# VectorE splits the routing's weights, the paced queue of GpSimd holds only issues, and the second half of the one-hot tables moves into the first pass over V

## The chip, the cores and the metric

The kernel runs on one core of one Trainium2 chip. Its engines are TensorE (PE, matmuls), VectorE (DVE), ScalarE (ACT), GpSimd (POOL) and SyncE (SP, which issues most DMAs). Each engine takes its own instructions strictly in the order in which the program was built, and waits for others by semaphores. The metric is the device time of one execution in microseconds, lower is better.

## The reference, cut to what matters

Two layers. Each has a token mixer (three attentions, projections), which the change leaves alone, and then PEER, the retrieval of experts, which holds all of the change. There are 512 latent tokens and 256 context tokens (tiles of 128 tokens: 0 to 3 latent, 4 and 5 context); the second layer computes the latent tokens alone.

```python
def peer(h, wq, subkeys, u, v):
    q = (h @ wq).reshape(t, 8, 2, 128)
    s = einsum('thpd,hpnd->thpn', q, subkeys)          # 128 row scores, 128 column scores
    s_top, i_top = top_k(s, 16)
    ...                                                # 16 best of the 16 x 16 sums, for each head
    gate = softmax(best)
    a = gelu(einsum('cd,chkd->chk', hc, u[ec]))        # u, v: 16384 x 1024
    w = gc * a
    return einsum('chk,chkd->cd', w, v[ec])
```

Each token picks 8 x 16 = 128 of 16384 experts. The kernel doesn't gather 128 rows of V for a token: it makes, for each tile of tokens, a dense table of weights (16384 experts x 128 tokens, zero where an expert is not picked) and multiplies it with all of V.

## The kernel before

**Stages of a layer's PEER.** (1) The first pass over U (`upass`, half 0, matmuls into `pw`): 64 iterations, each loads a block of 128 experts (512 KB), splits it into two float16 parts (ScalarE the high one, VectorE the low one, tile `hl`), and multiplies it with the tokens of the *dense* tiles: 24 matmuls of 512 columns in layer 0 (tiles 2, 3, 4, 5), of 384 in layer 1 (tiles 2, 3, 1). Beside it run the routing (`routing`: 32 blocks of queries a layer, `rw`, whose weights `wq` and `sk` are scaled and split in `wsplit`) and the choice of experts (`pick`, with 128 small VectorE instructions `gjk` a tile that has a table). (2) The second pass over U (half 1, into `pa`), 64 iterations of the same. (3) Two passes over V (`vpass`, into `acc`), 128 iterations each, for three tiles in layer 0 (18 matmuls of 512 columns an iteration) and two in layer 1 (12). V too is split into two `hl` parts, one iteration ahead of its use.

**Three kinds of work fill the passes**, put into each iteration by generators at hand-written rates (`RRATE` for the routing, `RATES` for the gathers, `SRATES` for the scatters, by layer and stage):
- *Gathers* (`gather`, L946): tiles that are not dense (0 and 1 in layer 0, 0 in layer 1) fetch their 128 picked rows of U for every token. GpSimd issues 128 indirect DMAs a tile (512 KB each, into one of three buffers `r`), and VectorE multiplies each row with the tokens' `h` and sums it (L952).
- *Scatters* (`Table.put`, L1248): the weights of tiles 4, 5, 0, 1 (layer 0) and 0, 1 (layer 1) go into their table in HBM by 128 indirect DMAs a tile from GpSimd, 16 for each head; the next head's wait until they have landed. The table must be full before the pass over V that reads it (`need`).
- *One-hot blocks* (`Onehot.block`): the weights of tiles 2 and 3 are made on the chip. 32 blocks for each half of the columns; a block is three VectorE instructions (`oi`, `oj`, `og`), 16 small matmuls, and for half 0 a VectorE product into `P`, for half 1 two ScalarE copies into `P`. Before, all 64 run in the second pass over U, one an iteration.

**What sets the order.** A scheduler places all instructions on the engines' queues by its own estimates of time and by the program's order. `queue_behind` adds an edge without a semaphore: a gather or scatter may not stand before `lo_ins`, the last split that GpSimd did. When the routing's last split has been written, `lo_ins` stays where it is, and nothing more holds the issues back.

In `gather`, `h` is copied by ScalarE into PSUM (`hp`), and the products are summed in `a` (two buffers).

## Time and profile before

| | us |
|---|---|
| median of 3 runs | 5107.54 (5106.78 to 5112.42) |
| the profiled execution | 5100.45 |
| its span, first instruction to last | 5098.7 |
| PE busy | 4160.3 (82%) |
| DVE busy | 3334.4 (65%) |
| ACT busy | 1935.6 (38%) |
| POOL busy | 1776.3 (35%) |

The busy shares are means over stages with different limits: where one engine is busy all the time another may be idle, and the stage's own rows say which. POOL's issue of an indirect DMA counts as busy; the transfer itself runs on the DMA engines afterwards.

### The profile page before, as it was taken

What the parts mean: (1) busy time and instruction counts of PE and PEld (TensorE: products, weight loads), DVE (VectorE), ACT (ScalarE), POOL (GpSimd) and SP (SyncE); (2) the same over time, 40 slices, a digit from 0 to 9 for tenths busy, and PEclk for the clock granted to TensorE, in tenths of its full rate; (3) what the DMA queues carried; (4) which work ended last, traced back from release to release, by engine and by line L of the source; (5) the groups of instructions that cost most, each with busy time, mean ns of one, the idle gap of its engine ahead of it and who ended that gap; (6) DMA issues with size and microseconds to landing.
All of it is one profiled execution on the core that took longest, in us unless ns stands there. A gap on an engine that the chain in (4) does not pass through costs nothing. (4 is left out here: it accounts for less than half of the span.)

```text
span 5098.7 us, 74857 instructions
## 1 busy us (share of the span) xinstructions
PE 4160.3 (82%) x27326; PEld 2297.0 (45%) x27326; DVE 3334.4 (65%) x7769; ACT 1935.6 (38%) x3191; POOL 1776.3 (35%) x1680
## 2 busy tenths in 40 slices
PE   4987898981687777799899989878866587899898
PEld 3664554740343333344344456646543354444343
DVE  6677559691786666655565544654976587667565
ACT  4556343420122222233333346644432123455444
POOL 3224133477456676620000012333257645400000
PEclk9996899995898889899999999879988798999999
DMA  7831443321477788897788842134543477668787
GB/s 254 298 102 34 150 131 98 116 76 31 153 250 247 250 281 262 272 324 239 241 265 257 252 134 81 43 113 138 172 144 116 143 238 254 226 218 254 254 274 237
DMA packets 512322, 971.54 MB, mean 191 GB/s; under 512 B 73824, under 2 KB 295488, under 8 KB 511952
## 3 DMA queue, kind: packets, MB, share of 16 engines
q1 hardware_dynamic: 422464, 759.66, 46.2%
...
HBM read 861.77 MB, written 104.78 MB: 190 GB/s over the span
## 5 line engine op out<-in xcount | busy, mean ns | idle before, releaser
L1126 PE MATMUL acc<-hl,gst 128*128 128x512 f16 x7680 | 1710.7, 385 | 152.5 <-DVE hl L1114 105.8
L1126 PEld LDWEIGHTS <-gst 128*128 128x128 f16 x7680 | 760.6, 99 | 1101.9 <-issue 217.9
L952 DVE SCALAR_TENSOR_TENSOR r<-r,hp 128x1024 f32<-128x1024 f32 x384 | 466.2, 1218 | 580.0 <-DMA r<-peer_u,ix 579.4
L1113 ACT ACTIVATE hl<-s 128x1024 f16<-128x1024 f32 x512 | 538.0, 1051 | 698.5 <-PE acc L1126 392.2
L1114 DVE TENSOR_TENSOR hl<-s,hl 128x1024 f16<-128x1024 f32 x512 | 626.3, 1224 | 244.8 <-ACT hl L1113 243.4
L946 POOL DMA_INDIRECT r<-peer_u,ix x384 | 421.9, 1099 | 488.9 <-DVE r L952 339.5
L168 PE MATMUL pa<-h2Uh,hl 128*128 128x512 f16 (+1 forms) x1024 | 384.2, 376 | 192.9 <-DVE hl L143 192.8
L160 POOL TENSOR_TENSOR rstd<-rstd,mhalf 128x1 f32<-128x1 f32 x26 | 14.2, 546 | 1352.1 <-DVE rstd L159 1348.2
L1248 POOL DMA_INDIRECT table<-a,to x384 | 428.9, 1117 | 149.7 <-issue 110.7
L1248 POOL DMA_INDIRECT table<-gs,to x384 | 410.4, 1069 | 188.1 <-issue 108.8
L168 PE MATMUL pw<-h2Uh,hl 128*128 128x512 f16 (+1 forms) x1024 | 376.4, 368 | 67.1 <-DVE hl L143 67.0
L143 DVE SCALAR_TENSOR_TENSOR hl<-s,hl 128x1024 f16<-128x1024 f32 x256 | 313.7, 1226 | 172.0 <-ACT hl L139 172.0
L168 PEld LDWEIGHTS <-hl 128*128 128x128 f16 x2048 | 209.9, 102 | 477.9 <-DVE hl L143 272.3
L166 PE MATMUL pa<-h2Uh,hl 128*128 128x512 f16 (+1 forms) x1024 | 387.8, 379 | 8.7 <-ACT hl L139 8.7
L166 PE MATMUL pw<-h2Uh,hl 128*128 128x512 f16 (+1 forms) x1024 | 376.9, 368 | 14.0 <-ACT gst L1054 13.7
L167 PE MATMUL pa<-h2Ul,hl 128*128 128x512 f16 (+1 forms) x1024 | 385.7, 377 | 0.0
L167 PE MATMUL pw<-h2Ul,hl 128*128 128x512 f16 (+1 forms) x1024 | 375.7, 367 | 0.0
L153 POOL TENSOR_TENSOR wl<-wst,wh 128x512 f16<-128x512 f32 x96 | 127.9, 1344 | 504.4 <-ACT wh L152 468.5
L167 PEld LDWEIGHTS <-hl 128*128 128x128 f16 x2048 | 210.8, 103 | 205.2 <-issue 52.8
L166 PEld LDWEIGHTS <-hl 128*128 128x128 f16 x2048 | 210.8, 103 | 204.5 <-issue 39.1
L168 PE MATMUL pj<-wh,hTl 128*128 128x256 f16 x1072 | 295.7, 276 | 1.9 <-DVE hTl L141 1.6
L166 PE MATMUL pj<-wh,hTh 128*128 128x256 f16 x1072 | 295.8, 276 | 1.3 <-ACT hTh L139 1.3
...
## 6 DMA issues: line engine op xcount, KB each, us to landing
s<-peer_v SPq DMA_DIRECT2D x512, 512.0 KB, 4.7
s<-ut SPq DMA_DIRECT2D x256, 512.0 KB, 4.1
...
wq<-peer_wq SPq DMA_DIRECT2D x128, 256.0 KB, 3.6
...
```

Source lines behind the costliest of these rows:

```text
L143: nc.vector.scalar_tensor_tensor(lo, src, scale, hi, op0=OP.mult, op1=OP.subtract)
L153: self.lo_ins = nc.gpsimd.tensor_tensor(lo, w, hi, op=OP.subtract)
L160: nc.gpsimd.tensor_tensor(r, r, self.mhalf[:, :w], op=OP.pow)
L166: nc.tensor.matmul(out, ah, bh, start=start, stop=False)
L167: nc.tensor.matmul(out, ah, bl, start=False, stop=False)
L168: nc.tensor.matmul(out, al, bh, start=False, stop=stop)
L946: self.queue_behind(nc.gpsimd.indirect_dma_start(out=r, out_offset=None, in_=self.i["peer_u"], in_offset=bass.IndirectOffsetOnAxis(ap=ix[: ...
L952: nc.vector.scalar_tensor_tensor(r, r, 1.0, hp, op0=OP.mult, op1=OP.mult, accum_out=a[:, d // 16, d % 16:d % 16 + 1])
L1113: nc.scalar.activation(vh[:, 0], v, AF.Copy)
L1114: nc.vector.tensor_tensor(vh[:, 1], v, vh[:, 0], op=OP.subtract)
L1126: nc.tensor.matmul(acc[s][hf], pr[:, w, s, j % 2], vh[:, x, hf * 512:hf * 512 + 512], start=j == 0 and i == 0, stop=j == 127 and i == 2)
L1248: ins = o.nc.gpsimd.indirect_dma_start(out=self.d, out_offset=bass.IndirectOffsetOnAxis(ap=to[:, k, h:h + 1], axis=0), in_=values[:, c + s ...
```

## The change

- `wsplit` takes an engine for the low part. The routing's low parts (`wql`, `skl`) go from GpSimd to VectorE. In the first 24 iterations of the first pass over U (`UPOOL`), the low part of U goes from VectorE to GpSimd, with one more ScalarE instruction that scales U.
- `lo_ins` is now the low split of U or V of each iteration, on whichever engine, so it moves on through all passes.
- `Onehot.blocks(half)`: half 0 is made in the second pass over U, one block in two iterations; half 1 in the first pass over V, one block in two iterations, until iteration 62.
- `h` of a gather stays in SBUF (`hg`), without the copy into PSUM; `a` and `hg` have one buffer each. The second pass over U has two PSUM buffers for four, `wq` two buffers for four, `sk` two for three, `oi` and `og` one for two. In layer 0's second pass over V both vectors of the next layer's `ada` stand in `r` buffers, before one stood in PSUM.
- New rates.

```diff
-RATES = {0: (1.0, 1.4, 1.4, 1.4, 0.0, 0.0), 1: (1.0, 1.0, 0.8, 0.8, 0.0, 0.0)}
-SRATES = {0: (2.5, 2.6, 1.7, 2.2, 4.0, 4.0), 1: (2.5, 2.5, 1.4, 1.6, 4.0, 4.0)}
-RRATE = (1.2, 1.0)
+RATES = {0: (0.8, 1.0, 1.5, 1.5, 0.0, 0.0), 1: (0.6, 1.2, 0.4, 0.8, 0.0, 0.0)}
+SRATES = {0: (2.0, 2.9, 1.6, 1.8, 4.0, 4.0), 1: (1.5, 1.8, 0.9, 1.2, 4.0, 4.0)}
+RRATE = (1.3, 1.05)
...
+UPOOL = 24
...
-        self.lo_ins = nc.gpsimd.tensor_tensor(lo, w, hi, op=OP.subtract)
+        return (lo_eng or nc.gpsimd).tensor_tensor(lo, w, hi, op=OP.subtract)
...
-            sk = pool.tile([128, 128], F32, name="sk", bufs=3)
+            sk = pool.tile([128, 128], F32, name="sk", bufs=2)
...
-            self.wsplit(skh, skl, sk, SKS)
+            self.wsplit(skh, skl, sk, SKS, lo_eng=nc.vector)
...
-                w = pool.tile([128, 4, 128], F32, name="wq", bufs=4)
+                w = pool.tile([128, 4, 128], F32, name="wq", bufs=2)
...
-                self.wsplit(wh, wl, w)
+                self.wsplit(wh, wl, w, lo_eng=nc.vector)
...
-        h = self.gp.tile([128, D], F32, name="r")
+        h = self.lp.tile([128, D], F32, name="hg", bufs=1)
         nc.scalar.dma_start(h, self.h2d[t])
-        hp = self.hpp.tile([128, D], F32, name="hp")
-        nc.scalar.activation(hp, h, AF.Copy)
-        a = self.lp.tile([128, 8, 16], F32, name="a", bufs=2)
+        a = self.lp.tile([128, 8, 16], F32, name="a", bufs=1)
...
-                nc.vector.scalar_tensor_tensor(r, r, 1.0, hp, op0=OP.mult, op1=OP.mult,
+                nc.vector.scalar_tensor_tensor(r, r, 1.0, h, op0=OP.mult, op1=OP.mult,
...
-            ps = self.pool(e, "ups", 4, space=PSUM)
+            ps = self.pool(e, "ups", 2, space=PSUM)
...
-                vec = [self.srow(r(), 0, self.hpp.tile([128, D], F32, name="hp")), self.srow(r(), 1)]
+                vec = [self.srow(r(), x) for x in range(2)]
...
-        steps = iter(self.onehot) if half else iter(())
+        steps = self.onehot.blocks(0) if half else iter(())
...
-            self.split(uh[:, 0], uh[:, 1], u, US)
+            if not half and jj < UPOOL:
+                self.lo_ins = self.wsplit(uh[:, 0], uh[:, 1], u, US)
+            else:
+                self.lo_ins = self.split(uh[:, 0], uh[:, 1], u, US)
...
-            if jj >= 1:
+            if jj % 2:
                 next(steps, None)
...
+                if j == 62:
+                    self.drain(steps)
...
-            nc.vector.tensor_tensor(vh[:, 1], v, vh[:, 0], op=OP.subtract)
+            self.lo_ins = nc.vector.tensor_tensor(vh[:, 1], v, vh[:, 0], op=OP.subtract)
...
+        steps = self.onehot.blocks(1) if n == 0 else iter(())
...
+            if j % 2:
+                next(steps, None)
```

**Place 1: GpSimd's queue at layer 0's first gathers**, at the end of the first pass over U (`r<-peer_u` is a gather, `table_4`, `table_5`, `table_0` are scatters of those tiles). Before:

```order
L1248 DMA table_4_102<-gs,to 2097152x1 x16
L1248 DMA table_5_103<-gs,to 2097152x1 x4
L1248 DMA table_4_102<-gs,to 2097152x1 x16
L1248 DMA table_5_103<-gs,to 2097152x1 x80
L946 DMA r<-peer_u,ix 128x1024 x3
L1248 DMA table_5_103<-gs,to 2097152x1 x32
L946 DMA r<-peer_u,ix 128x1024 x17
L1248 DMA table_0_100<-a,to 2097152x1 x3
```

With the change:

```order
L154 TENSOR_TENSOR hl<-s_9374,hl 128x1024
L1266 DMA table_4_102<-gs,to 2097152x1 x68
L946 DMA r<-peer_u,ix 128x1024
L1266 DMA table_4_102<-gs,to 2097152x1 x2
L946 DMA r<-peer_u,ix 128x1024
L1266 DMA table_4_102<-gs,to 2097152x1 x2
L946 DMA r<-peer_u,ix 128x1024
L1266 DMA table_4_102<-gs,to 2097152x1 x4
```

Before, 224 of the 256 scatters of the two context tiles (4 and 5) stood ahead of the first gather, and the last 32 ahead of the fourth; now 68 scatters of tile 4 stand ahead of the first gather, and from there on two to four stand between gathers.

**Place 2: GpSimd's queue where layer 0's second gathered tile (tile 1) follows the first (tile 0)**, in the first pass over V. Before:

```order
L946 DMA r<-peer_u,ix 128x1024 x3
L1248 DMA table_0_100<-a,to 2097152x1
L946 DMA r<-peer_u,ix 128x1024
L1248 DMA table_0_100<-a,to 2097152x1 x2
L946 DMA r<-peer_u,ix 128x1024 x3
L1248 DMA table_1_101<-a,to 2097152x1 x2
L946 DMA r<-peer_u,ix 128x1024
```

With the change:

```order
L946 DMA r<-peer_u,ix 128x1024
L1266 DMA table_0_100<-a,to 2097152x1 x32
L287 MEMSET zero 128x512
L1266 DMA table_0_100<-a,to 2097152x1 x17
L946 DMA r<-peer_u,ix 128x1024 x18
L1266 DMA table_1_101<-a,to 2097152x1 x2
L946 DMA r<-peer_u,ix 128x1024 x3
L1266 DMA table_1_101<-a,to 2097152x1
```

Before, gathers of the one tile passed into those of the next without a break; now the second tile's gathers begin behind the last scatter of the first tile, which in the built order stands beside iteration 69 of 128 of the pass (the one buffer `a` comes free there), and all 128 stand between iterations 70 and 125.

**Place 3: VectorE's queue late in that pass** (iterations 84 to 87; `hl` are V's low parts, on which TensorE waits, `gst` and `h2U` the weights). Before:

```order
L1114 TENSOR_TENSOR hl<-s_21765,hl 128x1024
L1114 TENSOR_TENSOR hl<-s_21793,hl 128x1024
L1088 TENSOR_TENSOR h2Ul<-P,h2Ul 128x512
L1091 TENSOR_TENSOR h2Ul<-h2Ul 128x256
L141 TENSOR_TENSOR gst<-h2Uh,gst 128x768
L1114 TENSOR_TENSOR hl<-s_21832,hl 128x1024
```

With the change:

```order
L1128 TENSOR_TENSOR hl<-s_21694,hl 128x1024
L952 SCALAR_TENSOR_TENSOR r,a<-r,hg 128x1024
L1096 TENSOR_TENSOR h2Ul<-P,h2Ul 128x512
L952 SCALAR_TENSOR_TENSOR r,a<-r,hg 128x1024
L1099 TENSOR_TENSOR h2Ul<-h2Ul 128x256
L1128 TENSOR_TENSOR hl<-s_21729,hl 128x1024
L952 SCALAR_TENSOR_TENSOR r,a<-r,hg 128x1024 x2
L142 TENSOR_TENSOR gst<-h2Ul,gst 128x768
L952 SCALAR_TENSOR_TENSOR r,a<-r,hg 128x1024
L1128 TENSOR_TENSOR hl<-s_21760,hl 128x1024
```

Where no gather stood before, two or three now stand ahead of each `hl`.

## Rows read from the trace of the kernel before

**Rows 1.** Stages: start:end, length, busy PE, PEld, DVE, ACT, POOL (instructions), PEclk, DMA.

```profile
613.50:1154.20 540.70, 493.15 (x4114) 297.16 (x4112) 414.47 (x2132) 209.28 (x413) 247.41 (x233) 0.95 0.35 107
1154.20:1355.90 201.70, 57.27 (x296) 24.99 (x295) 65.91 (x251) 16.65 (x23) 123.94 (x126) 0.64 0.21 62
1355.90:1812.00 456.10, 360.66 (x2289) 167.78 (x2288) 345.39 (x684) 107.67 (x186) 275.25 (x250) 0.90 0.76 246
1812.00:2206.00 394.00, 289.99 (x1150) 120.62 (x1150) 259.00 (x411) 99.25 (x141) 266.74 (x240) 0.89 0.82 274
2206.00:2478.00 272.00, 249.40 (x1155) 112.92 (x1154) 146.92 (x172) 99.25 (x111) 24.77 (x19) 0.96 0.82 274
2478.00:2978.00 500.00, 499.41 (x2304) 225.70 (x2303) 307.81 (x385) 183.17 (x190) 0.00 (x0) 1.00 0.78 247
3433.40:3913.90 480.50, 372.60 (x3246) 251.22 (x3244) 347.76 (x1559) 190.08 (x408) 209.96 (x198) 0.91 0.48 149
3913.90:4043.00 129.10, 50.48 (x316) 27.88 (x315) 46.20 (x83) 16.67 (x25) 99.01 (x96) 0.68 0.28 81
4043.00:4386.00 343.00, 269.98 (x2274) 166.74 (x2272) 269.59 (x431) 101.35 (x184) 176.72 (x164) 0.90 0.77 249
4386.00:4733.60 347.60, 333.89 (x1536) 150.70 (x1536) 230.33 (x246) 169.70 (x197) 22.18 (x19) 0.98 0.72 228
```

**Rows 2.** Waits, 1154.2 to 1355.9 (who <- whom: total us, times, longest).

```profile
PE pa L168 <- DVE hl L143: 137.6, 3, 106.4
DVE r L952 <- DMA r<-peer_u,ix: 135.8, 2, 105.1
```

**Rows 3.** Timeline of POOL at two heads' first scatters, 16 issues apart.

```profile
1199.77 0.96 POOL L1248 DMA_INDIRECT table<-gs,to  x1 [2.17 <-issue]
...
1221.84 0.96 POOL L1248 DMA_INDIRECT table<-gs,to  x1 [2.17 <-issue]
```

**Rows 4.** Waits in layer 1, 3913.9 to 4043.

```profile
DVE r L952 <- DMA r<-peer_u,ix: 82.8, 6, 45.3
...
PE pa L168 <- DVE hl L143: 48.0, 2, 43.1
```

**Rows 5.** Groups, 1356 to 1812: busy us, mean ns, idle before.

```profile
L952 DVE SCALAR_TENSOR_TENSOR r<-r,hp 128x1024 f32<-128x1024 f32 x127 | 154.4, 1218 | 106.0 <-DMA r<-peer_u,ix 105.7
...
L143 DVE SCALAR_TENSOR_TENSOR hl<-s,hl 128x1024 f16<-128x1024 f32 x56 | 68.3, 1220 | 0.0
...
L1198 DVE TENSOR_TENSOR og<-oj,gT 128x1024 f16<-128x1024 f16 x59 | 40.6, 688 | 0.0
L1194 DVE TENSOR_TENSOR oi<-iox,sT 128x1024 f16<-128x1024 f16 x59 | 40.5, 686 | 0.0
...
L1194 DVE TENSOR_TENSOR oj<-iox,sT 128x512 f16<-128x512 f16 x59 | 24.9, 422 | 0.0
...
L1213 DVE TENSOR_TENSOR P<-pw,P 128x512 f32<-128x512 f32 x27 | 18.6, 688 | 4.0 <-PE pw L1205 4.0
```

**Rows 6.** Groups by form, 613.5 to 1154.2.

```profile
L919 DVE SCALAR_TENSOR_TENSOR gjk<-ef,sgate 128x128 bf16<-128x128 f32 x374 | 106.6, 350 | 0.0
...
L153 POOL TENSOR_TENSOR wql<-wq,wqh 128x512 f16<-128x512 f32 x60 | 74.0, 1252 | 194.2 <-ACT wqh L152 107.3 <-PE rw L168 86.9
...
L151 ACT ACTIVATE wq<-wq 128x512 f32<-128x512 f32 x56 | 35.2, 630 | 117.2 <-DMA wq<-peer_wq 114.5 <-POOL skl L153 2.7
```

**Rows 7.** Groups by form, 1812 to 2206.

```profile
L952 DVE SCALAR_TENSOR_TENSOR r<-r,hp 128x1024 f32<-128x1024 f32 x119 | 143.8, 1218 | 127.2 <-DMA r<-peer_u,ix 127.0
```

**Rows 8.** Timeline: two VectorE instructions and the POOL issues that overlap them.

```profile
1860.84 1.22 DVE L1114 TENSOR_TENSOR hl<-s,hl 128x1024 f16<-128x1024 f32 x1
1861.10 1.82 POOL L946 DMA_INDIRECT r<-peer_u,ix  x1 [0.30 <-DVE r L952]
...
1862.43 1.22 DVE L952 SCALAR_TENSOR_TENSOR r<-r,hp 128x1024 f32<-128x1024 f32 x1
1863.22 0.96 POOL L946 DMA_INDIRECT r<-peer_u,ix  x1 [0.30 <-issue]
```

More of the change, by code (lines that the diff above doesn't have):

```diff
@@ L716, in first @@
                     self.mm3(p, yT[0][:, k], yT[1][:, k], wh, wl, k == 0, k == KC - 1)
-                v = pool.tile([128, 512], F32, name="wov")
+                v = pool.tile([128, 512], F32, name="wov", bufs=1)
                 nc.vector.tensor_tensor(v, p, self.mod2[:, c:c + 512], op=OP.mult)
@@ L909, in pick @@
         if t in self.picked:
-            ix = self.lp.tile([128, 16, 8], I32, name="ix", bufs=2)
+            ix = self.lp.tile([128, 16, 8], I32, name="ix", bufs=len(self.picked))
             nc.vector.tensor_scalar(ix, ef, float(l * 16384), None, op0=OP.add)
@@ L970, in peer @@
         nc = self.nc
-        self.hpp = self.pool(es, "hp", 1, space=PSUM)
         self.gp = self.pool(es, "gat", 3)
@@ L990, in peer @@
                 self.step(self.rg, 1)
+        pws.close()
+        self.pw = self.pool(es, "ohp", 2, space=PSUM)
         h2s.close()
@@ L1045, in upass @@
             uh = uhs.pop(0)
-            pa = ps.tile([128, 512], F32, name=tag)
+            pa = ps.tile([128, nd * 128], F32, name=tag)
             for k in range(KC):
-                self.mm3(pa[:, :nd * 128], uh[:, 0, k], uh[:, 1, k], hh[:, k], hl[:, k], k == 0, k == KC - 1)
+                for i, (x, h) in enumerate(((0, hh), (0, hl), (1, hh))):
+                    for c in range(0, nd * 128, 512):
+                        d = min(c + 512, nd * 128)
+                        nc.tensor.matmul(pa[:, c:d], uh[:, x, k], h[:, k, c:d], start=k == 0 and i == 0,
+                                         stop=k == KC - 1 and i == 2)
             if not half:
@@ L1106, in load @@
             if j % 2 == 0:
-                self.pr = self.weigh(tiles, j, *gs.pop(0))
+                *w, self.spare = gs.pop(0)
+                self.pr = self.weigh(tiles, j, *w)
+                if j == 62:
+                    self.drain(steps)
                 if j + 2 < 128:
                     gs.append(self.weights(tiles, j + 2))
-            v = self.vp.tile([128, D], F32, name="s4", bufs=3)
+            if j % 2 and self.spare is not None:
+                v = self.spare
+            else:
+                v = self.vp.tile([128, D], F32, name="s4", bufs=self.nv)
             vh = self.vp.tile([128, 2, D], F16, name="hl", bufs=3)
@@ L1138, in vpass @@
         for s, t in enumerate(tiles):
-            x = self.vp.tile([128, D], F32, name="s4", bufs=3)
+            x = self.vp.tile([128, D], F32, name="s4", bufs=self.nv)
             self.load_x(x, t)
-            v = self.vp.tile([128, D], F32, name="s4", bufs=3)
+            v = self.vp.tile([128, D], F32, name="s4", bufs=self.nv)
             for hf in range(2):
@@ L1177, in prep, with blocks @@
         self.sT[t] = sT, gT
-    def __iter__(self):
-        for half in range(2):
-            for s in range(2):
-                for tb in range(0, 128, TB):
-                    self.block(half, s, tb)
-                    yield
+    def blocks(self, half):
+        for s, t in enumerate(self.tiles):
+            while t not in self.sT:
+                self.o.step(self.o.rg, 1)
+            for tb in range(0, 128, TB):
+                self.block(half, s, tb)
+                yield
     def block(self, half, s, tb):
@@ L1188, in block @@
         sT, gT = self.sT[self.tiles[s]]
-        oi = o.sp.tile([128, TB, 128], F16, name="oi")
+        oi = o.sp.tile([128, TB, 128], F16, name="oi", bufs=1)
         oj = o.sp.tile([128, TB, 64], F16, name="oj", bufs=1)
-        og = o.sp.tile([128, 2, TB, 64], F16, name="og")
+        og = o.sp.tile([128, 2, TB, 64], F16, name="og", bufs=1)
         ioj = o.iox[:, half * 64:half * 64 + 64]
```

19 lines of the change are left out of this document (10 added, 9 removed).

## The prediction

> **What bounds the kernel now.** I read the stretches of the span first [rows 1], since the whole-span shares average over stages with different limits. In the passes TensorE is the bound wherever nothing disturbs it: layer 0's second V pass (2478 to 2978) has 499.4 us of TensorE work in 500, so one matmul of 512 columns costs 499.4/2304 = 0.217 us, 24 of them (an iteration of layer 0's U passes) 5.2 us, 18 (V pass, or layer 1's U passes in 384 columns) 3.9, and 12 (layer 1's V passes) 2.6. Against this the second U pass is far off: 1154.2 to 1355.9 holds 57 us of TensorE work in 201.7, and 3913.9 to 4043 holds 50 in 129.1, with the clock granted at 0.64 and 0.68 (a mean over the two levels, since the engine had stood idle in these stretches; before, at 0.95 and 0.91). Those are the two holes.
>
> Second, the waits inside the holes. In layer 0 TensorE waits 137.6 us for `hl`, VectorE's low part, 106.4 at a stretch, while VectorE waits 135.8 us at L952 for a gathered row [rows 2]. VectorE's queue is in order: the multiplication of a row that has not arrived stands ahead of U's split. Layer 1 has the same pair, 82.8 and 48.0 us [rows 4]. Why the row is late: GpSimd has 224 scatters ahead of the first gather (place 1), and a head's 16 issues take 1221.84 - 1199.77 = 22.07 us, 1.38 an issue, though a row shows 0.96 of it busy [rows 3]. I price issues at 1.38. Beyond the hole the wait goes on: VectorE waits another 105.7 us for rows in 1356 to 1812 [rows 5] and 127.0 in 1812 to 2206 [rows 7], where TensorE has only 361 of 456 us and 290 of 394 [rows 1].
>
> **The change, part by part.** The sum is made against the profiled execution's 5100.45 us; the median, 5107.54, is 7.1 above it and is added to at the end.
>
> *First U pass, both layers: +20 us.* VectorE gives up 24 low parts at 1.22 (the price at L143 [rows 5]), 29 us, and takes 64 `wql`. Their price on VectorE is not in the trace: it lies between 0.69 (same shape, L1213 [rows 5]) and GpSimd's 1.25 [rows 6]; I take 0.69, so 44 us, and some 6 for 32 `skl`. VectorE is busy 414 of 541 us and TensorE 493 [rows 1], so 20 us more on VectorE is covered; without that cover it would cost its 20 us. The 24 low parts cost GpSimd about 2.5 us each (twice 1.25 for twice the width) and ScalarE 1.3 (twice 0.63 [rows 6]), on engines busy 247 and 209 of 541 us. What may not be covered is latency: ScalarE already waits 114.5 us for `wq` to arrive with four buffers [rows 6], and with two the next load starts only when VectorE has finished a split that may stand behind a run of `gjk`. I give it 20 us for both layers together, a third of a us for each of the 64 blocks. Below: a quarter of TensorE's idle time in the two stages (48 and 108 us [rows 1]) could vanish, -40; above, 2 us a block, +130.
>
> *Layer 0, hole and second U pass: -250.* From here gathers and scatters alternate (place 1), held to the iteration they were written in, so the 100 us wait has no cause. VectorE's work in the first eight iterations is then the load: a tile's 128 `gjk` at 106.6/374 = 0.285 [rows 6] is 36.5, eight splits and six multiplications at 1.22, 17, four one-hot blocks at 0.69 + 0.42 + 0.69 + 0.69 = 2.49 [rows 5], 10: 64, say 66 us. In the other 56 iterations the rates ask of GpSimd 1.0 gather and 2.9 scatters each, 3.9 x 1.38 = 5.4 us, which is above TensorE's 5.2: GpSimd becomes the pace. To it comes the multiplication's `h`, now in SBUF. In [rows 8] an issue takes 1.82 us when it lies under `hl<-s,hl`, which reads two tiles from SBUF, and 0.96 under today's multiplication, which reads one from PSUM. So each multiplication may delay an issue by 0.86 us if they meet; from below nothing, if they don't; from above its whole 1.22. I take 0.4, half of 0.86, as GpSimd issues nothing for some of the time. 5.8 us, with 5% for the bursts 6.1, x 56 = 342. In all 408, for 657.8 before (201.7 + 456.1).
>
> The Trainium skill ("SBUF — State Buffer", section "SBUF: two separate sides") says that the port pair that VectorE shares with GpSimd is locked by a VectorE instruction with two SBUF inputs, against a GpSimd operation that reads SBUF, for the whole instruction, and that the other fully blocks. The trace agrees in part: an issue under `hl<-s,hl` took 1.82 and not 0.96 us. By this rule moving `h` out of PSUM is a loss of up to 1.22 us a multiplication, which is a rival below: 5051 us by the rule, 4844 by my reading of the row.
>
> *Layer 0's first V pass: +82* (394 + 272 = 666 before, its end with the change of pass included). Here the change takes back something. Tile 1's gathers start only when `a` is free, at iteration 70, and then all 128 gathers and some 124 scatters must be issued by iteration 125 (place 2), where before the second half had 19 instructions on GpSimd [rows 1]. In the built order tile 0's last gathers end by iteration 38. For these 38 iterations VectorE has 1.8 us of other work ((259.0 - 143.8)/64 [rows 1, 7]), 1.5 multiplications, 1.8 us, and half a one-hot block of half 1 (0.69 + 0.42 + 0.69 = 1.8, so 0.9): 4.5, less 0.1 as fewer `gst` parts wait, plus 8% is 4.8, x 38 = 182. 26 more without gathers at TensorE's 3.9 plus 10%: 111. Six at 3.9: 24. Then 252 issues x 1.38 = 348 us for 56 iterations whose TensorE work is 218, plus 128 x 0.4 = 51 for the lock, 15 for bursts, and 17 for the last scatters, behind which the next pass's table read waits: 431. Together 748. In this last part VectorE's queue (place 3) has two or three multiplications ahead of each `hl`, so a late row makes TensorE late.
>
> *Layer 0's second V pass: +5.* One `ada` vector moves from PSUM to an `r` buffer, which leaves one buffer of three for its stream of weights; TensorE is full there [rows 1], so cover is thin. From 0 to 30.
>
> *Layer 1, hole and second U pass: -155.* 129.1 + 343 = 472.1 before. First eight iterations 40 (as in layer 0, with TensorE's 3.9 an iteration and fewer `gjk`). Then 1.2 + 1.8 = 3.0 issues at 1.38, 4.1, + 1.2 x 0.4 for the lock = 4.6, + 7% = 4.95, x 56 = 277. In all 317.
>
> *Layer 1's first V pass: +34.* Today 347.6 with TensorE busy 334 [rows 1]. VectorE's 230.33/128 = 1.8, + 0.4 x 1.22 for gathers, + 0.9 for one-hot blocks = 3.15, above TensorE's 2.6: 64 x 3.15 = 201; the other 64 at 2.6, 166; 15 for scatters that end late: 382.
>
> The other edits (buffers `sk`, `oi`, `og`, two PSUM buffers in the second U pass) I cost at nothing: `oi` and `og` are made in order on one engine and read by 16 short matmuls in an iteration of 5 us. If that cover is gone, 2 us for each of the 128 blocks, 256 us, which I hold unlikely since a block now has two iterations to itself.
>
> **Sum:** 20 - 250 + 82 + 5 - 155 + 34 = -264; 5100.45 - 264 = 4836, and 7.1 more for the median: **4844 us**. The lock at 0.4 is in it 253 times in GpSimd-bound stretches (101 us). Its own range is 4740 (no lock) to 4930 (the four plus terms a third larger, 47, and 40 more on the first U pass).
>
> **Rivals.**
> - *Cheaper still, 4700.* No lock (-101), and the 5 to 8% I put on for bursts (some 45 us) vanish, since rows arrive in time. For it: an issue is only 0.96 us busy [rows 3]. Against: 16 issues in a row took 1.38 each.
> - *The lock takes the whole multiplication, 5051.* 1.22 for 0.4 at 253 places is +207. For it, 1.82 against 0.96 [rows 8]; against, that one shows 0.86 and not 1.22, and only when they meet.
> - *Slower: the first U pass starves on its routing, 5144.* Two `wq` buffers, their split on VectorE behind `gjk` and U's split, and TensorE's in-order queue behind `rw`: if a block waits x us, 64 blocks cost 64x, and the sign turns at 264/64 = 4.1 us a block. At 5 us (320, for my 20) it is 4844 + 300 = 5144. For it, the 114.5 us wait for `wq` [rows 6]; against, a block is spread over about two iterations, 10 us.
> - *The change doesn't do what it says, 5103.* GpSimd's issues come slower than 1.38 when gathers and scatters alternate. At 2.0 us, lock included, the second U pass needs 56 x 3.9 x 2.0 = 437 us for my 342, layer 0's last 252 issues 504 for my 399, layer 1's 56 x 3.0 x 2.0 = 336 for my 277: +259, 5103. The wait for rows is then only spread. For it, 1.82 us in [rows 8]; against, 1.38 as the mean of 16 in [rows 3].
>
> **How the numbers follow.** The forecast 0.63, cheaper 0.15, whole lock 0.10, slower 0.07, no change 0.05. A measurement of this kernel tells 0.2%, 10 us, from nothing. The slower case and a quarter of the last are slower, 0.08; most of the rest of the last is the same, 0.04; faster 0.88. The range runs from the cheaper case to just short of the whole lock, 4690 to 5030: outside it lie the two last cases, part of the lock's, and a little of the cheapest.
>
> **What the changed profile would show.** Right: no wait of VectorE at L952 above some 20 us at the start of either second U pass, and no TensorE wait for `hl` there; the second U pass of layer 0 near 408 us with GpSimd the busiest queue; its first V pass longer than 666, with GpSimd full in the last third; issues under L952 longer than 1.0 us. Wrong: a first U pass over 600 us with TensorE waiting for `wql`; L952 waits as large as before, only spread; issues under L952 at 0.96 (no lock) or near 2 us.

## The result and the profile after

The change takes 4921.92 us (median of 4, 4918.54 to 4932.08), the kernel before 5107.16 beside it: 0.964, 95% interval 0.9623 to 0.9656. So 185 us were gained, where 263 were forecast; the time lies inside the range. The profiled execution took 4932.08 us, with a span of 4930.0, so the traces show 169 us of difference and not 185.

The stretches of the changed kernel, cut at the first matmul of a pass (columns as in [rows 1]): layer 0's first U pass, the first eight iterations of the second, its other 56, the first V pass in three pieces (38, 26 + 6 and 58 iterations), then layer 1's first U pass, its second in the same two pieces and its first V pass.

```profile
610.90:1186.10 575.20, 502.35 (x4135) 300.97 (x4134) 473.75 (x2309) 231.16 (x439) 149.16 (x110) 0.93 0.35 108
1186.10:1260.70 74.60, 45.96 (x257) 21.25 (x256) 64.45 (x304) 13.94 (x19) 37.34 (x26) 0.82 0.40 126
1260.70:1628.50 367.80, 322.55 (x1797) 148.97 (x1794) 200.61 (x294) 87.41 (x117) 271.81 (x233) 0.95 0.70 208
1628.50:1830.10 201.60, 174.66 (x988) 79.86 (x989) 160.80 (x265) 66.97 (x116) 146.91 (x112) 0.91 0.81 266
1830.10:1966.30 136.20, 132.58 (x791) 62.70 (x787) 86.00 (x126) 54.37 (x89) 68.61 (x60) 0.99 0.72 226
1966.30:2441.20 474.90, 288.62 (x1046) 111.95 (x1045) 279.19 (x416) 95.06 (x111) 320.46 (x259) 0.80 0.81 273
...
3405.10:3874.60 469.50, 379.00 (x3272) 255.74 (x3270) 376.99 (x1641) 212.72 (x434) 128.47 (x90) 0.91 0.47 144
3874.60:3907.70 33.10, 33.10 (x258) 20.66 (x256) 23.00 (x33) 11.81 (x18) 20.32 (x16) 1.00 0.77 244
3907.70:4201.80 294.10, 245.55 (x1798) 146.88 (x1794) 210.96 (x317) 84.59 (x120) 224.93 (x173) 0.94 0.81 263
4201.80:4566.70 364.90, 349.74 (x2048) 165.71 (x2049) 302.18 (x393) 188.27 (x261) 178.22 (x129) 0.98 0.79 258
```

The two holes of [rows 1] are gone: layer 0's first eight iterations take 74.6 us with 46 us of TensorE work, layer 1's 33.1, all of it TensorE work with the clock granted at 1.00. What is new is the piece 1966.3 to 2441.2: 58 iterations in 474.9 us, TensorE busy 289 of them at a granted clock of 0.80 (a mean over its two levels, 1.2 and 2.4 GHz, in a stretch in which it stood idle 186 us). Before, the second half of that pass ran at 0.96 and took 272 us [rows 1].

The waits in the first eight iterations (who waits for whom, total, times, longest), to be read beside [rows 2]: the wait for a gathered row fell from 135.8 us to 11.3, TensorE's for `hl` from 137.6 to 23.4.

```profile
PE pa L1054 <- DVE hl L144: 23.4, 1, 23.4
...
DVE r L952 <- DMA r<-peer_u,ix: 11.3, 3, 8.7
```

### The profile page after: what moved, and what is told of

Same layout as the page of the kernel before. It is cut to its first block, busy times and chain, and to the rows that moved or that the text cites. A ratio compares the mean times of both kernels' runs of the same rounds, so it can differ in the third digit from the quotient of the medians.

```text
span 4930.0 us, 74817 instructions
## 1 busy us (share of the span) xinstructions
PE 4154.8 (84%) x27326; PEld 2287.3 (46%) x27326; DVE 3391.1 (69%) x7913; ACT 1981.4 (40%) x3236; POOL 1877.5 (38%) x1536
## 5 line engine op out<-in xcount | busy, mean ns | idle before, releaser
L1127 ACT ACTIVATE hl<-s 128x1024 f16<-128x1024 f32 x512 | 538.4, 1053 | 748.0 <-PE acc L1141 393.9
L952 DVE SCALAR_TENSOR_TENSOR r<-r,hg 128x1024 f32<-128x1024 f32 x384 | 468.7, 1224 | 458.1 <-DMA r<-peer_u,ix 457.1
L946 POOL DMA_INDIRECT r<-peer_u,ix x384 | 481.8, 1255 | 665.6 <-DVE r L952 240.0
L1054 PE MATMUL pw<-h2Uh,hl 128*128 128x512 f16 (+1 forms) x2048 | 601.9, 371 | 83.4 <-DVE hl L144 71.0
L1054 PE MATMUL pa<-h2Uh,hl 128*128 128x512 f16 (+1 forms) x2048 | 584.2, 363 | 49.7 <-DVE hl L144 49.4
L1266 POOL DMA_INDIRECT table<-a,to x384 | 494.0, 1286 | 172.4 <-issue 122.3
L1266 POOL DMA_INDIRECT table<-gs,to x384 | 470.1, 1224 | 201.9 <-issue 128.8
L168 PE MATMUL pj<-wl,hTh 128*128 128x256 f16 x1072 | 296.0, 276 | 0.0
L1061 ACT ACTIVATE gst<-pa 128x512 f32<-128x512 f32 (+1 forms) x128 | 69.5, 543 | 486.2 <-PE pa L1054 383.7
L140 ACT ACTIVATE hl<-s 128x1024 f16<-128x1024 f32 x208 | 219.1, 1053 | 11.8 <-DMA s<-ut 10.7
L154 POOL TENSOR_TENSOR hl<-s,hl 128x1024 f16<-128x1024 f32 x48 | 106.3, 2218 | 290.0 <-ACT hl L153 264.5
```

What stands on the lines that cost most here:

```text
L154: return (lo_eng or nc.gpsimd).tensor_tensor(lo, w, hi, op=OP.subtract)
L168: nc.tensor.matmul(out, ah, bl, start=False, stop=False)
L946: self.queue_behind(nc.gpsimd.indirect_dma_start(out=r, out_offset=None, in_=self.i["peer_u"], in_offset=bass.IndirectOffsetOnAxis(ap=ix[: ...
L952: nc.vector.scalar_tensor_tensor(r, r, 1.0, h, op0=OP.mult, op1=OP.mult, accum_out=a[:, d // 16, d % 16:d % 16 + 1])
L1054: nc.tensor.matmul(pa[:, c:d], uh[:, x, k], h[:, k, c:d], start=k == 0 and i == 0, stop=k == KC - 1 and i == 2)
L1127: nc.scalar.activation(vh[:, 0], v, AF.Copy)
```

## The stages in all kernels

Stages in us, in one profiled execution. They are cut by count: a stage begins with the matmul that follows as many as the stages ahead of it hold. In the kernels with the old loop of the pass (before, 2, 10 and 12), and in layer 1 of experiment 1, the first 3 to 12 matmuls of the second U pass stand in TensorE's queue ahead of the last of the first, so there this cut lies 9 to 21 us behind the second pass's first matmul (1163.7 for 1154.2 and 3926.9 for 3913.9 in the kernel before). Experiments 1 to 4 ran on a chip where the kernel before took 5281.72 us, all others where it took 5100 to 5107, so a kernel is compared with those of its own chip.

| kernel | L0 U1 | L0 U2 | L0 V1 | L0 V2 and mixer | L1 U1 | L1 U2 | L1 V1 | span |
|---|---|---|---|---|---|---|---|---|
| before | 550.1 | 648.3 | 666.1 | 955.3 | 493.5 | 459.2 | 347.5 | 5098.7 |
| change | 575.3 | 442.4 | 812.7 | 963.9 | 469.5 | 327.2 | 364.9 | 4930.0 |
| 5 change again | 572.0 | 432.4 | 805.2 | 958.9 | 471.5 | 323.4 | 364.3 | 4901.8 |
| 6 first pass undone | 566.9 | 427.2 | 800.7 | 951.8 | 473.6 | 326.6 | 364.0 | 4892.5 |
| 7 all one-hot in U2 | 572.0 | 440.2 | 793.7 | 965.2 | 472.0 | 333.7 | 357.0 | 4909.2 |
| 8 two `a`, rates | 574.7 | 433.0 | 767.0 | 960.9 | 471.4 | 321.6 | 365.9 | 4875.2 |
| 9 change, third | 572.1 | 430.7 | 811.3 | 963.3 | 471.7 | 329.5 | 364.8 | 4918.0 |
| 10 before + pacing | 550.5 | 431.5 | 684.5 | 952.7 | 486.6 | 344.8 | 363.6 | 4788.2 |
| 11 two `a`, old first pass | 567.4 | 465.7 | 722.8 | 952.7 | 461.1 | 330.2 | 365.5 | 4842.4 |
| 12 as 10, new rates in L1 | 553.6 | 428.2 | 685.7 | 954.4 | 467.1 | 312.9 | 358.4 | 4737.3 |
| *first chip:* 1 unpaced | 825.7 | 620.5 | 650.5 | 961.3 | 560.1 | 441.1 | 360.4 | 5391.7 |
| 2 before + pacing | 599.7 | 469.0 | 693.5 | 952.1 | 503.4 | 391.8 | 360.7 | 4950.9 |
| 3 two `a` | 614.6 | 431.4 | 747.9 | 963.6 | 476.1 | 326.0 | 364.3 | 4897.6 |
| 4 `h` in PSUM, L1 | 610.9 | 452.9 | 815.0 | 958.0 | 477.9 | 333.9 | 369.8 | 4998.0 |

## The experiments

The theory was that holding the gathers and scatters to the iteration that wrote them (the pacing) closes the holes, and that the rest of the change costs something back in layer 0's first V pass. The rivals were that the moved one-hot blocks, the new rates or the swap of engines in the first pass bring the gain.

**1. The change without the pacing.**

```diff
-                self.lo_ins = self.wsplit(uh[:, 0], uh[:, 1], u, US)
+                self.wsplit(uh[:, 0], uh[:, 1], u, US)
...
-            self.lo_ins = nc.vector.tensor_tensor(vh[:, 1], v, vh[:, 0], op=OP.subtract)
+            nc.vector.tensor_tensor(vh[:, 1], v, vh[:, 0], op=OP.subtract)
...
-                self.wsplit(wh, wl, w, lo_eng=nc.vector)
+                self.lo_ins = self.wsplit(wh, wl, w, lo_eng=nc.vector)
```

> The changed kernel, with one part undone: the splits of U and V no longer move the mark that gathers and scatters must stand behind, only the routing's splits do. In the built order 222 scatters again stand ahead of layer 0's first gather, and 61 in a row ahead of one at the end of layer 1's first U pass. Theory (the pacing closes the holes): at 1.38 us an issue the waits for rows return at the start of both second U passes, some 100 and 80 us, while tile 1's gathers, which now come early, give back up to 60 in layer 0's first V pass: about 5040 us (4980 to 5110). Rival (the moved one-hot blocks and the new rates closed the holes): 4920 us, within 20.

Measured: 5388.68 us, 1.0187 of before (1.0152 to 1.0222), far above what either said. The gain is gone, and the interval lies above 1. Beside experiment 4, which has the change's layer 0 on the same chip, layer 0's second U pass is 168 us longer and the first V pass 165 shorter; layer 1's second U pass is 115 us longer than in experiment 3, whose layer 1 is the change's. But the hole at the start did not come back in layer 0. Its first eight iterations take 68.5 us (73.2 in experiment 4): the 222 scatters run inside the first U pass here, and the first gather is issued at 1358.4 us, ahead of the second pass's start at 1435.1. The loss lies in the other 56 iterations, 552.0 us for 379.7. VectorE waits 196.6 us for rows in the pass (119.9 in experiment 4), in pieces of at most 8.8 us, and TensorE 126.0 for `og`, which stands behind them (18.3):

```profile
PE pw L1222 <- DVE og L1216: 126.0, 24, 9.6
```

```profile
DVE r L952 <- DMA r<-peer_u,ix: 196.6, 74, 8.8
```

What no theory had is the first U pass, 825.7 us for 610.9, and in layer 1 560.1 for 477.9. This is the timeline there, GpSimd and TensorE, and then the same 40 us as a window:

```profile
1062.06 0.96 POOL L1266 DMA_INDIRECT table<-gs,to  x1 [0.30 <-issue]
1063.33 0.96 POOL L1266 DMA_INDIRECT table<-gs,to  x1 [0.30 <-issue]
1064.59 0.96 POOL L1266 DMA_INDIRECT table<-gs,to  x1 [0.30 <-issue]
```

```profile
1062.91 0.27 PE L167 MATMUL rw<-h2T,wqh 128*128 128x128 f16 x1 [3.23 <-issue]
1065.71 0.27 PE L168 MATMUL rw<-h2T,wqh 128*128 128x128 f16 x1 [2.54 <-issue]
1067.82 0.26 PE L169 MATMUL rw<-h2T,wql 128*128 128x128 f16 x1 [1.84 <-issue]
1070.61 0.27 PE L167 MATMUL rw<-h2T,wqh 128*128 128x128 f16 x1 [2.53 <-issue]
```

```profile
1060.00:1100.00 40.00, 3.71 (x14) 1.44 (x14) 0.00 (x0) 0.00 (x0) 28.50 (x30) 0.50 0.02 1
```

While scatters follow one another without a break, TensorE starts one matmul of 0.27 us every 2 to 3 us, 14 in 40 us, and waits for nothing that the profile shows ("issue"); VectorE and ScalarE do nothing. Whether that comes from the chip or from the kernel is told by experiment 4, which has the change's layer 0. The same 50 us of a run of scatters, first the change on the chip of the result, then experiment 4 on this one:

```profile
860.00:910.00 50.00, 45.51 (x425) 29.20 (x424) 50.00 (x305) 13.88 (x26) 35.65 (x32) 0.93 0.29 85
```

```profile
860.00:910.00 50.00, 18.78 (x113) 9.13 (x111) 25.03 (x155) 3.20 (x6) 33.40 (x35) 0.63 0.05 9
```

With the same instructions in the same order, TensorE is busy 45.5 us on the one chip and 18.8 on the other. So on this chip a long run of scatters is itself the price, beside the late rows behind it. The kernel before was not traced on this chip; that this is why it is 175 us slower here fits, and is not shown.

**2 and 10. The kernel before with the pacing and nothing else**, first on that chip, then beside the change on one of the others. `split` returns its instruction, and two lines keep it.

```diff
-            self.split(uh[:, 0], uh[:, 1], u, US)
+            self.lo_ins = self.split(uh[:, 0], uh[:, 1], u, US)
...
-            nc.vector.tensor_tensor(vh[:, 1], v, vh[:, 0], op=OP.subtract)
+            self.lo_ins = nc.vector.tensor_tensor(vh[:, 1], v, vh[:, 0], op=OP.subtract)
```

> The kernel before, with the one part alone: the low splits of U and V move the mark, all else as before (old rates, h in PSUM, all one-hot blocks in the second U pass, two buffers a). Theory (pacing): the stretch that held the holes loses 130 to 200 us in layer 0 and about 100 in layer 1: about 4860 us (4800 to 4950), lower than the whole change, since tile 1's gathers run on without a break. Rival (pacing alone does little, VectorE's full load of one-hot blocks keeps the second U pass long): above 5000 us.

Measured: 4954.11 us, 0.937 of before (0.9338 to 0.9403), 4 us above the theory's range, on the chip where the kernel before takes longer too.

> The kernel before with the pacing alone, as in the second experiment, now beside the change. Theory (the pacing brings the whole gain, the rest of the change moves work about): within 30 us of the change on either side; on the stages, layer 0's first V pass some 100 us shorter than the change's (two buffers a), both second U passes together some 90 us longer (all one-hot blocks and higher rates there). Rival (the rest brings a good part): 50 us or more above the change.

Measured: 4809.53 us, 0.9432 of before (0.9416 to 0.9448), and 4809.53 / 4918.06 = 0.978 of the change on the same chip (experiment 9). The two lines bring 295 us, and neither statement held: the rest of the change is no gain, it costs 109 us. By the table the change loses 127 us to experiment 10 in layer 0's first V pass, 22 in its first U pass and 11 in its second V pass with the mixer, and gains 30 in layer 1's U passes. Windows of experiment 10: first eight iterations of layer 0's second U pass, its other 56, and the second half of the first V pass.

```profile
1152.10:1217.90 65.80, 53.37 (x295) 23.51 (x294) 65.80 (x251) 16.66 (x23) 28.60 (x25) 0.92 0.53 167
1217.90:1593.10 375.20, 331.75 (x2289) 158.56 (x2288) 293.95 (x593) 105.68 (x181) 261.38 (x236) 0.97 0.75 236
1905.40:2277.60 372.20, 276.63 (x1154) 118.13 (x1153) 241.78 (x342) 103.20 (x119) 253.60 (x222) 0.89 0.90 316
```

The hole of 201.7 us [rows 1] is 65.8, cut at the pass's first matmul as there, shorter than the change's 74.6, though VectorE has all one-hot blocks to make there and is busy all of the time. The first gather is issued at 1116.7 us behind 92 scatters, in the kernel before at 1264.1 behind 224. Tile 1's gathers run on without a break, and the V pass's second half takes 372.2 us, with the clock at 0.89.

**3. The change with two buffers `a`.**

```diff
-        a = self.lp.tile([128, 8, 16], F32, name="a", bufs=1)
+        a = self.lp.tile([128, 8, 16], F32, name="a", bufs=2)
```

> The changed kernel with two buffers a for one, nothing else. In the built order tile 1's gathers now follow tile 0's from iteration 40 of layer 0's first V pass on, for 70. Theory (the single buffer squeezes 128 gathers into 56 iterations, where rows are late and the clock falls): the pass falls from 813 us to 650 to 720, the whole to about 4810 us (4770 to 4860). Rival (the pass is bound by the sum of GpSimd's and VectorE's work, wherever it stands): 4920 us, within 15.

Measured: 4905.62 us, 0.9281 of before (0.9245 to 0.9317). Experiment 4, on the same chip and with the change's layer 0, has 815.0 us in layer 0's first V pass, this one 747.9: 67 us for a buffer of 512 bytes a partition. The theory holds, with less than it said: the pass did not reach 720. By pieces, the last 58 iterations take 364.7 us for 471.3, the 32 ahead of them 175.6 for 140.1.

**4. `h` in PSUM again in layer 1.**

```diff
+        if l:
+            hp = self.hpp.tile([128, D], F32, name="hp")
+            nc.scalar.activation(hp, h, AF.Copy)
+            h = hp
```

> The changed kernel, but in layer 1 h is copied to PSUM again (in layer 0 there is no room beside the sums and the one-hot blocks), so layer 0 is its own control. Theory (the shared port costs some 0.4 us a multiplication): issues that meet a multiplication in layer 1 fall from 1.1 us or more to 0.97, and layer 1's second U pass, with about 69 of them, gains 28 us: about 4895 us. Rival 1 (the whole multiplication blocks): 84 us less, 4840. Rival 2 (the issues have slack there): no change, 4920 within 8.

Measured: 4996.36 us, 0.9443 of before (0.9402 to 0.9484); layer 1's second U pass 333.9 us, against 326.0 in experiment 3, whose layer 1 is the change's. Groups in that pass, experiment 3 and then this one (busy us, mean ns, idle before):

```profile
L1266 POOL DMA_INDIRECT table<-gs,to x84 | 109.7, 1306 | 39.8 <-issue 26.1 <-DMA table<-gs,to 13.7
...
L946 POOL DMA_INDIRECT r<-peer_u,ix x76 | 94.0, 1236 | 34.9 <-issue 17.2 <-DVE r L952 12.9 <-DVE hl L144 3.0
...
L1266 POOL DMA_INDIRECT table<-a,to x31 | 39.6, 1276 | 10.8 <-issue 8.5 <-DMA table<-a,to 2.2
```

```profile
L1272 POOL DMA_INDIRECT table<-gs,to x84 | 97.1, 1156 | 42.2 <-issue 26.8 <-DMA table<-gs,to 15.4
...
L950 POOL DMA_INDIRECT r<-peer_u,ix x76 | 88.4, 1163 | 60.4 <-DVE r L956 38.1 <-issue 18.5 <-DMA table<-gs,to 3.2
...
L1272 POOL DMA_INDIRECT table<-a,to x32 | 36.6, 1143 | 11.1 <-issue 9.4 <-DMA table<-a,to 1.7
```

The port's price is there: an issue falls from 1236 to 1163 ns, and from 1306 and 1276 to 1156 and 1143. In all 243.3 us against 222.1, 21.2 us for 77 multiplications, 0.28 each. Sorted by what VectorE does meanwhile, an issue beside no VectorE instruction takes 0.98 us in both kernels, and one that overlaps a multiplication 1.38 us on average in experiment 3 (112 issues) and 1.11 here (93). But the time does not follow: GpSimd waits longer for a buffer `r` to come free (12.9 to 38.1 us). Rival 2 is right for layer 1's time, the theory for the issue. The whole can't be set beside the 4920 us of the statement, since this chip's first U pass alone is 36 us longer.

**5 and 9. The change again.** No edit.

> The change itself, unaltered, beside the others of this call and the kernel before. In the call ahead of this one the kernel before took 5281.72 us where it had taken 5107.16, so ratios across calls don't compare. Theory (that chip loses time where scatters are issued without a break, and the change has fewer of them): where before takes about 5280 the change takes 4960 to 4990, 0.94; where it takes 5107, 4922, 0.964. Rival (that chip is slower everywhere): 0.964 at any time of before.

> The change itself once more, so that the three others can be set beside it on one chip. Where the kernel before takes about 5100 us: 4908 to 4922, 0.964. Where it takes about 5280: 4985, 0.944.

Measured: 4907.73 us, 0.9634 of before (0.9609 to 0.966), and 4918.06, 0.9644 (0.9626 to 0.9663). Both ran on chips where before takes 5100, so what the change takes on the other stays open.

**6. The first pass as before**, with the small buffers kept.

```diff
-            self.wsplit(skh, skl, sk, SKS, lo_eng=nc.vector)
+            self.wsplit(skh, skl, sk, SKS)
...
-                self.wsplit(wh, wl, w, lo_eng=nc.vector)
+                self.wsplit(wh, wl, w)
...
-UPOOL = 24
+UPOOL = 0
```

> The changed kernel with the routing's low parts on GpSimd again and U's low parts all on VectorE; wq and sk keep their two buffers. Theory (the first U pass as forecast: VectorE loses and gains about as much, layer 0 a little longer, layer 1 a little shorter): within 15 us of the change. Rival 1 (the swap is a loss in the first U pass): 25 us or more below the change, in layer 0's first U pass. Rival 2 (the swap frees the pick of experts and lets gathers begin early): 25 us or more above it.

Measured: 4888.32 us, 0.9575 of before (0.9548 to 0.9602), 19 us below experiment 5. The profiled executions differ by 9 us: 5 of them lie in layer 0's first U pass, and the other stages differ by 2 to 7 us in either direction, in stages that the edit touches only through the order. The swap gains nothing; it lies between the theory and rival 1.

**7. All one-hot blocks in the second U pass.**

```diff
-        steps = self.onehot.blocks(0) if half else iter(())
+        steps = itertools.chain(self.onehot.blocks(0), self.onehot.blocks(1)) if half else iter(())
...
-            if jj % 2:
-                next(steps, None)
+            next(steps, None)
...
-        steps = self.onehot.blocks(1) if n == 0 else iter(())
+        steps = iter(())
```

> The changed kernel with all 64 one-hot blocks in the second U pass again, one an iteration, and none in the first V pass. Theory (the move trades time between the passes, and gains little): the second U passes grow by 20 us in layer 0 and 30 in layer 1, the first V passes fall by 30 and 15: within 25 us of the change. Rival (VectorE is the pace of the second U pass when all blocks stand there): 60 us or more above the change, as the paced kernel before, with all blocks in the U pass, has 27 us more there in layer 0 and 64 in layer 1.

Measured: 4914.36 us, 0.9635 of before (0.9604 to 0.9665), no different from the change. The stages trade: +8 and -12 us in layer 0, +10 and -7 in layer 1. The theory holds for the whole, with less than half of the trade that it said.

**8. Two buffers `a` and higher rates in layer 0's first V pass.**

```diff
-RATES = {0: (0.8, 1.0, 1.5, 1.5, 0.0, 0.0), 1: (0.6, 1.2, 0.4, 0.8, 0.0, 0.0)}
+RATES = {0: (0.8, 1.0, 1.6, 1.7, 0.0, 0.0), 1: (0.6, 1.2, 0.4, 0.8, 0.0, 0.0)}
-SRATES = {0: (2.0, 2.9, 1.6, 1.8, 4.0, 4.0), 1: (1.5, 1.8, 0.9, 1.2, 4.0, 4.0)}
+SRATES = {0: (2.0, 2.9, 1.7, 2.4, 4.0, 4.0), 1: (1.5, 1.8, 0.9, 1.2, 4.0, 4.0)}
```

> The changed kernel with two buffers a, and with higher rates in layer 0's first V pass (gathers 1.6 and 1.7 an iteration for 1.5, scatters 1.7 and 2.4 for 1.6 and 1.8), so that the last scatter of tile 1 stands at iteration 119 and not behind 127. Theory (the end of that pass waits for the last scatters, 89 us in its last eight iterations): the pass falls from 813 to 700 to 730 us, the whole 80 to 115 us below the change of this call. Rival (denser issues only move the waits forward): 50 to 70 us below, as with two buffers alone.

Measured: 4863.02 us, 0.9527 of before (0.95 to 0.9555), 45 us below experiment 5. The last eight iterations fell from 88.9 to 47.9 us, but the second half's others took 46 to 59 us for eight, where experiment 3's took 39 to 48 (on the other chip): the pass is 767.0. The theory's 80 us were not reached, and the rival is nearer, though 45 is below its 50 too: denser issues moved the waits forward. Two buffers alone were not run on this chip, so what the rates bring by themselves is not shown.

**11. Two buffers `a`, the old first pass, and nearly the old rates in layer 0.**

```diff
-RATES = {0: (0.8, 1.0, 1.5, 1.5, 0.0, 0.0), 1: (0.6, 1.2, 0.4, 0.8, 0.0, 0.0)}
+RATES = {0: (1.0, 1.3, 1.4, 1.4, 0.0, 0.0), 1: (0.6, 1.2, 0.4, 0.8, 0.0, 0.0)}
-SRATES = {0: (2.0, 2.9, 1.6, 1.8, 4.0, 4.0), 1: (1.5, 1.8, 0.9, 1.2, 4.0, 4.0)}
+SRATES = {0: (2.5, 2.7, 1.7, 2.2, 4.0, 4.0), 1: (1.5, 1.8, 0.9, 1.2, 4.0, 4.0)}
```

(and the edits of 3 and 6)

> The changed kernel with two buffers a, the first U pass as before (routing's low parts on GpSimd, U's all on VectorE), and for layer 0 the rates before for gathers and scatters, but for 1.3 and 2.7 in the second U pass. Its last scatter of tile 1 stands at iteration 125. Theory (the parts add: 45 us for a and the end of the pass, 19 for the first pass): 60 to 90 us below the change, some 4840 us where before takes 5100. Rival (they are worth the same microseconds, as the transfers of a pass are the limit): 45 below.

Measured: 4855.21 us, 0.9522 of before (0.9505 to 0.9539), 63 us below the change, at the low end of what the theory said. That the parts add is not shown, since the rates moved work too: layer 0's second U pass is 35 us longer than in experiment 9, its first V pass 89 shorter, its first U pass 5 shorter.

**12. The kernel before with the pacing, and the change's rates for layer 1.**

```diff
-RATES = {0: (1.0, 1.4, 1.4, 1.4, 0.0, 0.0), 1: (1.0, 1.0, 0.8, 0.8, 0.0, 0.0)}
+RATES = {0: (1.0, 1.4, 1.4, 1.4, 0.0, 0.0), 1: (0.6, 1.2, 0.4, 0.8, 0.0, 0.0)}
-SRATES = {0: (2.5, 2.6, 1.7, 2.2, 4.0, 4.0), 1: (2.5, 2.5, 1.4, 1.6, 4.0, 4.0)}
+SRATES = {0: (2.5, 2.6, 1.7, 2.2, 4.0, 4.0), 1: (1.5, 1.8, 0.9, 1.2, 4.0, 4.0)}
```

(and the edit of 2)

> The kernel before with the pacing, and the change's rates for layer 1 alone; all one-hot blocks in the second U pass, h in PSUM, two buffers a. Theory (in layer 1 the new rates, not the moved blocks, make the second U pass shorter): layer 1's second U pass falls from 391 us to 340, the whole 40 us below the paced kernel with old rates. Rival (the moved blocks do it): within 10 us of that kernel.

Measured: 4738.95 us, 0.9283 of before (0.9263 to 0.9303), 71 us below experiment 10. Layer 1's second U pass takes 312.9 us with all one-hot blocks in it, 32 less than in experiment 10 and less than in the change: the rates do it, not the moved blocks. It is the fastest kernel here, 179 us below the change. So the change's other parts hold a gain of some 71 us, layer 1's rates, and losses that outweigh it.

## Why the prediction was right, and where its sizes were off

The terms, forecast and measured between the profiled executions of before and of the change, in us. The stages are cut as the forecast cut them, at the first matmul of each pass (1154.2 and 3913.9 for before), so the U passes differ from the table of stages, which has +25, -206, -24 and -132.

| term | forecast | measured |
|---|---|---|
| first U passes | +20 | +35 and -11 |
| layer 0, hole and second U pass | -250 | -215 |
| layer 0, first V pass | +82 | +147 |
| layer 0, second V pass (measured with layer 1's mixer) | +5 | +9 |
| layer 1, hole and second U pass | -155 | -145 |
| layer 1, first V pass | +34 | +17 |
| the rest of the span | 0 | -4 |
| sum | -264 | -169 |

Each term came out with the sign that was forecast, and the total lies in the range, 78 us above the forecast. Of the 95 us that the terms miss together, 65 are layer 0's first V pass.

**The holes.** Right in cause and in kind: the pacing takes the run of scatters away, and the pacing alone, without any other part, takes 217 us off layer 0's second U pass and 114 off layer 1's (experiment 10, by the table of stages). The rest of the change takes nothing more off the first, and 15 off the second, which experiment 12 gives to the rates.

**Layer 0's second U pass** was said to go at GpSimd's pace, and it does. Groups in its last 56 iterations:

```profile
L1266 POOL DMA_INDIRECT table<-gs,to x156 | 184.9, 1185 | 72.8 <-issue 51.4 <-DMA table<-gs,to 19.5 <-DMA r<-peer_u,ix 1.8
...
L952 DVE SCALAR_TENSOR_TENSOR r<-r,hg 128x1024 f32<-128x1024 f32 x59 | 72.2, 1224 | 166.6 <-DMA r<-peer_u,ix 166.6
L946 POOL DMA_INDIRECT r<-peer_u,ix x61 | 71.5, 1172 | 18.6 <-issue 15.9 <-DVE hl L144 1.2 <-DVE oj L1212 0.9
...
L1266 POOL DMA_INDIRECT table<-a,to x16 | 17.1, 1070 | 4.9 <-issue 4.6 <-DMA table<-a,to 0.3
```

GpSimd issues 156 + 61 + 16 = 233 times in 367.8 us, 1.58 us each, and 6.1 / 3.9 = 1.56 was forecast. Its own queue fills the time: 272 us busy and 72 of "issue" between the issues, and only 20 us wait for scatters to land. What was mis-sized is the number: 233 for 56 x 3.9 = 218; that the 15 more are issues that the first iterations had put off is not shown. They are 15 x 1.56 = 23 us of the 35 missed (442.4 for 408), and 9 are in the first eight iterations (74.6 for 66). VectorE still waits 166.6 us for rows here, no less than the 105.7 of [rows 5], but in pieces of at most 7.7, and TensorE is busy 323 us of 368.

**Layer 0's first V pass** is the term with the largest error, 812.7 us for 748. Where the forecast had 182, 135 and 431 for its three parts, it took 201.6, 136.2 and 474.9. Groups in the last part:

```profile
L1141 PE MATMUL acc<-hl,gst 128*128 128x512 f16 x1046 | 289.4, 441 | 186.3 <-ACT gst L140 128.3 <-DVE hl L1128 42.2 <-DVE gst L142 15.6
L946 POOL DMA_INDIRECT r<-peer_u,ix x125 | 157.7, 1262 | 117.1 <-DVE r L952 83.6 <-issue 18.0 <-DVE hl L1128 7.7
L952 DVE SCALAR_TENSOR_TENSOR r<-r,hg 128x1024 f32<-128x1024 f32 x128 | 156.1, 1224 | 159.9 <-DMA r<-peer_u,ix 159.8
L1266 POOL DMA_INDIRECT table<-a,to x128 | 156.0, 1219 | 47.2 <-issue 41.8 <-DMA table<-a,to 5.5
```

The term that was mis-sized most is "252 issues x 1.38 ... for 56 iterations", with GpSimd as the pace. GpSimd issues 253 times, but is idle 117.1 us before gathers, 83.6 of it until VectorE frees a buffer `r`, and VectorE waits 159.8 us for rows: with three buffers, each side waits for the other. The forecast had 15 us for such waits. TensorE idles 186 us of 475 and its clock is granted at 0.80, so a matmul takes 288.6 / 1046 = 0.276 us of busy time for 0.217. And the end was larger than the 17 us given to it: GpSimd's last scatter, then TensorE's first matmul of the next pass, in the timeline

```profile
2434.62 0.96 POOL L1266 DMA_INDIRECT table<-a,to  x1 [0.30 <-issue]
2435.88 0.96 POOL L1266 DMA_INDIRECT table<-a,to  x1 [0.30 <-issue]
```

```profile
2395.20 9.38 PE L1141 MATMUL acc<-hl,gst 128*128 128x512 f16 x29 [7.24 <-DVE gst L142]
2441.19 9.01 PE L1141 MATMUL acc<-hl,gst 128*128 128x512 f16 x31 [36.61 <-ACT gst L140]
```

36.6 us, in which `h2U` of the next pass waits for the table. The single buffer `a` is shown to make the last 58 iterations long (experiment 3: 107 us less there, 67 in the pass; with the rates of experiment 8 on the other chip 38 in the pass). It does not make the wait at the end, which two buffers alone leave as it was, in experiment 3:

```profile
2404.38 7.99 PE L1141 MATMUL acc<-hl,gst 128*128 128x512 f16 x28 [38.14 <-ACT gst L140]
```

With the higher rates of experiment 8 the last eight iterations fall from 88.9 to 47.9 us, so the end hangs on where the last scatters stand. The first 38 iterations missed by 20 us; no run tells why.

**Layer 1's first V pass** was forecast at +34 and measured at +17. Experiment 12 has +11 of it without the moved blocks, and moving the blocks back takes 7 off (experiment 7), so the blocks cost far less than the 64 x (3.15 - 2.6) = 35 us that the sum hung on them.

**The lock.** Of the forecast's 0.4 us a multiplication, 0.28 was measured in layer 1 (experiment 4). Over the whole kernel it comes out the same way: the issues of experiment 9 (the change) and then of experiment 10 (`h` in PSUM), from the two pages.

```profile
L946 POOL DMA_INDIRECT r<-peer_u,ix x384 | 485.8, 1265 | 679.1 <-DVE r L952 253.5
...
L1266 POOL DMA_INDIRECT table<-a,to x384 | 491.5, 1280 | 170.4 <-issue 124.5
L1266 POOL DMA_INDIRECT table<-gs,to x384 | 455.1, 1185 | 197.4 <-issue 123.1
```

```profile
L946 POOL DMA_INDIRECT r<-peer_u,ix x384 | 439.1, 1144 | 349.4 <-DVE r L952 135.0
L1248 POOL DMA_INDIRECT table<-gs,to x384 | 422.3, 1100 | 227.8 <-issue 110.8
L1248 POOL DMA_INDIRECT table<-a,to x384 | 440.3, 1147 | 180.4 <-issue 120.2
```

1432.4 - 1301.7 = 130.7 us, by 384 multiplications 0.34 each, though here one-hot blocks and other work lie differently too. So as a mean over all multiplications the whole lock (1.22 each) is out, and the 0.86 and nothing that bounded the term too. In neither pair did taking the price away shorten the second U pass: experiment 10 needs 375.2 us for its 56 iterations, the change 367.8. By the Trainium skill ("SBUF — State Buffer", section "SBUF: two separate sides") the other side blocks fully for the whole instruction; the traces agree that the issue pays, but the measured mean of 0.28 to 0.34 of a 1.22 us instruction is what decides here.

**The first U pass.** The sum of the two layers, +24, fits the +20 by luck: the forecast had a loss in both, and layer 1 gains. By the table of stages layer 0 loses 25 us and layer 1 gains 24. In layer 0 the paced kernel with four `wq` buffers needs 550.5 us there, the change 572.1, and undoing the swap of engines takes back only 5. The other 16 lie with the two `wq` and `sk` buffers, the routing's rate of 1.3 or another small part; no run tells them apart. What the forecast feared, that the next `wq` comes late, is not in the trace: ScalarE waits 46.8 us for it, 114.5 before [rows 6]. TensorE waits for VectorE there, 37.5 us for `hl` and 15.2 for `st` (27.2 and 8.1 before). Most of layer 1's -24 comes with its rates: experiment 12 against 10 has -20 (486.6 to 467.1), and the pacing alone has -7.

**The rivals.** Slower through the routing: layer 0's pass grew by 25 us in all, 0.4 us for each of 64 blocks, where 4.1 would have turned the sign. No change: the issue price is 1.58 us, not 2.0. Cheaper still: no, but kernels of that kind exist: the pacing alone takes 4810 us, with layer 1's new rates 4739.

**The signs.** VectorE's wait at the start (11.3 us), a first V pass longer than 666 and issues longer than 1.0 us beside a multiplication came as said. Three did not: TensorE still waits 23.4 us for `hl` at the start, the second U pass is 442 us and not 408, and GpSimd is not full in the V pass's last part (320 of 475 us). A sign of being wrong came in part: over the hole and the second U pass VectorE waits 178 us for rows, 241 before, only spread; the time fell all the same, as TensorE no longer stands for 100 us behind one of them.

What stays open: of the 72 us by which experiment 11 is behind experiment 10 in layer 0's second U and first V pass (1188.5 and 1116.0), how much is `h` in SBUF, how much the single `oi` and `og` and the two PSUM buffers, how much the rates.
